# Attention of a two-layer diffusion block: fixed program order, slots per unit, keys before values

## The chip, the cores and the metric

One core of a Trainium2 chip runs the whole program in one launch. The metric is the device time of one execution in microseconds (us), the median over several executions.

## What is computed

A block of two layers works on 512 noisy latent tokens and, in the first layer only, on 256 context tokens, with 1024 channels in fp32. Each layer makes one input projection and splits it into branches; the branch that the change touches is the attention, with 8 heads of 64 channels:

```python
def context_attention(q, k, v):
    s = jnp.einsum('bqhd,bkhd->bhqk', q, k).astype(jnp.float32) * (NA_HEAD_DIM ** -0.5)
    p = jax.nn.softmax(s, axis=-1).astype(v.dtype)
    return jnp.einsum('bhqk,bkhd->bqhd', p, v)
```

A latent query sees a window of 8 x 16 latent positions, with a bias by relative position and rotary q and k, and all 256 context keys in the same softmax; a context query sees the context alone. The other branches are a pooling over windows (A) and a gating unit u * (W_s LN(v) + b) on chunks of 128 positions (B). The three branches are projected, merged by gates, projected again and added to the stream; a squared-ReLU MLP follows.

## The kernel before

Every product is made of three fp32r matmuls (high x high, high x low, low x high), so a weight or an activation is first split into two parts: ScalarE copies the high part (`cp`, L127) and VectorE subtracts it from the value (`sub`, L121). Tokens lie along the free axis: an input projection of one block of 128 channels (`proj`, L451) is 24 pairs of matmuls, one of 512 columns for the latents and one of 256 for the context; where the context isn't needed (q and gates in the second layer) the second one is left out.

The attention takes the heads in four pairs. A unit is one block of 128 queries of one pair: four latent and two context units per pair in the first layer (24 units), four latent ones in the second (16 units). A latent unit goes through these steps:

- `scores`: 12 matmuls on 64 rows (L696) into a PSUM tile of two banks; on VectorE a maximum over the context part (L704), for each of the two heads the bias added with a running maximum (L708), and the sign turned (L710); on ScalarE two exponentials (L712); on VectorE the reciprocal (L714) and the scaling (L716, one per head).
- `turn`: 8 transposes of the weights (L728) in two PSUM banks, and of each the copy (L127) and the subtraction (L121).
- `values`: 8 matmuls (L743), then two copies (L127) and four additions (L752, L753).

A context unit has 6 matmuls of scores, 4 transposes and 4 matmuls of values, and no bias.

While one pair's units run, the projections of the next pair's values, keys and queries (in this order) run between them. `stream` yields them in chunks of six matmuls, and `fill(t)` takes chunks for t us. What these projections leave to do: the rotary step `rope_in` (four ScalarE copies, L640, that exchange halves of the heads; POOL L641 and L645, VectorE L644; the split), the transposes of the values (`v_out`, L625, in the one-bank ring `xring` that the transposes and the values' products of the units use too), the bias tables (`bias_make`, six POOL additions, L679, fed by 16 transfers of `bias_load`), and the second parts of the weights' splits. Part of it stands in the queue `bulk`, of which `drain(SLOT)` takes some 1.9 us of work once per unit, in the midst of `scores`. After the last pair's projections the stream makes six gates. The scheduler of the tile framework is free to move instructions within each engine's program against the order in which they are written. Branch B's product (`gate_mix`, L524) and branch A's (`pool_out`, L512) stand ahead of the attention, behind the projections of u.

## Time and profile before

| | us |
|---|---|
| three timed runs | 1980.58 median (1973.89 to 1982.14) |
| the profiled execution | 1971.65 |
| its span on the core | 1969.9 |
| TensorE busy (PE) | 1924.8, 98% of the span, 11298 instructions |
| VectorE busy (DVE) | 1113.8, 57% |
| ScalarE busy (ACT) | 780.7, 40% |
| GpSimd busy (POOL) | 91.2, 5% |
| chain that ended last | PE 85%, DVE 5%, ACT 5%, issue 2%, POOL 1%, DMA 1% |

The chain goes back from the last instruction, at each step to what released it, and tells which engine the end waits for. Busy time of PE is an upper bound of its work, because a matmul that waits in the pipe counts as busy. In the profile the attention of the first layer lies from about 137 to 335 us and that of the second from about 1254 to 1394 us; the openings with u, branch A and branch B stand just ahead of each.

### The profile page before, as it was taken

The numbers are of one execution on the slowest core, as the hardware profiler recorded it, in microseconds if no ns is written. First come the engines' busy times: TensorE is split into PE (matmuls) and PEld (weight loads), VectorE is DVE, ScalarE is ACT, GpSimd is POOL, SyncE is SP. The second block draws the span as 40 slices with busy tenths as digits, with TensorE's granted clock in tenths as the row PEclk, the third lists the DMA queues.
The fourth block names the chain that finished last, engine by engine and source line by source line (L and its number), as shares of the span: only waits on it lengthen the run. The fifth ranks groups of instructions, "written<-read, shape, count | busy, mean of one in ns | idle before, by whom it ended". The sixth has DMA issues, their size and how long they took to land.

```text
span 1969.9 us, 27864 instructions
## 1 busy us (share of the span) xinstructions
PE 1924.8 (98%) x11298; PEld 1657.4 (84%) x11298; DVE 1113.8 (57%) x1865; ACT 780.7 (40%) x1197; POOL 91.2 (5%) x94
## 2 busy tenths in 40 slices
PE   7999999999999999999999999999999999999998
PEld 3887778888888888888888898777888898989898
DVE  6747676755554565644544467577633554434356
ACT  5535565212133431422413445566422443424253
POOL 0023210000000000000000000341000000000000
PEclk9999899999999999999999999999999999999999
DMA  8222111433342333333343334121232222222324
GB/s 324 70 71 75 43 34 44 128 125 125 126 150 65 109 127 123 125 128 128 129 129 123 102 118 133 47 86 44 75 97 97 96 96 89 94 96 97 96 90 136
DMA packets 63440, 206.25 MB, mean 105 GB/s; under 512 B 7888, under 2 KB 14032, under 8 KB 63312
## 3 DMA queue, kind: packets, MB, share of 16 engines
q1 hardware_dynamic: 63312, 204.48, 31.6%
q8 instruction: 89, 1.46, 0.3%
q14 instruction: 39, 0.32, 0.0%
HBM read 202.35 MB, written 2.10 MB: 104 GB/s over the span
## 4 chain that ended last, share of the span: by engine, by line
PE 85%; DVE 5%; ACT 5%; issue 2%; POOL 1%; DMA 1%; SPq 0%; POOLq 0%; DVEq 0%; ACTq 0%
PE psum L237 68%; PE psum L451 11%; ACT arena_r L127 2%; DVE arena_r L121 1%; PE psum L728 1%; PE psum L743 1%; ACT arena_f L640 1%; PE psum L394 1%; PE psum L696 1%; DMA arena_f<-in_w_mod 1%; ACT arena_f L712 1%; ACT arena_f L127 1%; DVE arena_f L716 1%; POOL arena_f L679 1%; DVE arena_f L118 1%
## 5 line engine op out<-in xcount | busy, mean ns | idle before, releaser
L237 PE MATMUL psum<-arena_r 128*128 128x512 f32 (+1 forms) x8016 | 1370.3, 333 | 1.6 <-DVE arena_f L882 0.9
L237 PEld LDWEIGHTS psum<-arena_r 128*128 128x128 f32 x8016 | 1209.6, 188 | 159.5 <-DVE arena_r L121 1.6
L127 ACT ACTIVATE arena_r<-arena_f 128x1024 fp32r<-128x1024 f32 (+4 forms) x393 | 371.4, 950 | 985.1 <-PE psum L237 782.1
L121 DVE TENSOR_TENSOR arena_r<-arena_f,arena_r 128x1024 fp32r<-128x1024 f32 (+4 forms) x393 | 426.7, 1088 | 274.2 <-ACT arena_r L127 257.3
L451 PE MATMUL psum<-arena_r 128*128 128x512 f32 x1776 | 368.4, 357 | 0.0
L451 PEld LDWEIGHTS psum<-arena_r 128*128 128x128 f32 x1776 | 286.5, 190 | 45.7 <-issue 0.4
L911 DVE SCALAR_TENSOR_TENSOR arena_f<-psum,arena_f 128x512 f32<-128x512 f32 (+1 forms) x128 | 78.3, 633 | 256.1 <-PE psum L237 256.0
L263 DVE SCALAR_TENSOR_TENSOR arena_f<-arena_f 128x1024 bf16<-128x1024 f32 x128 | 156.5, 1222 | 1.4
L963 DVE COPY arena_f<-psum 128x2 f32<-128x2 f32 x64 | 10.3, 160 | 186.9 <-PE psum L237 186.9
L118 DVE TENSOR_TENSOR arena_f<-arena_f 128x768 f32<-128x768 f32 (+8 forms) x103 | 70.0, 681 | 17.4 <-ACT arena_f L274 14.2
L121 DVE TENSOR_TENSOR arena_r<-psum,arena_r 128x512 fp32r<-128x512 f32 (+2 forms) x96 | 61.5, 653 | 19.7 <-ACT arena_r L127 18.5
L127 ACT ACTIVATE arena_r<-psum 128x512 fp32r<-128x512 f32 (+2 forms) x96 | 53.7, 570 | 45.6 <-PE psum L728 25.3
L127 ACT ACTIVATE arena_f<-psum 64x128 f32<-64x128 f32 (+5 forms) x119 | 49.9, 435 | 48.8 <-PE psum L743 19.4
L966 ACT ACTIVATE arena_f<-arena_f 128x512 f32<-128x512 f32 x96 | 59.4, 651 | 11.3 <-DVE arena_f L124 11.3
L712 ACT ACTIVATE arena_f<-psum,arena_f 128x512 f32<-128x512 f32 (+1 forms) x80 | 50.9, 642 | 28.5 <-DVE arena_f L710 28.3
L696 PE MATMUL psum<-arena_r 64*128 64x256 f32 x432 | 48.3, 308 | 7.5 <-ACT arena_f L712 5.4
L728 PE MATMUL psum<-arena_f 128*128 128x128 f32 x288 | 46.2, 285 | 9.0 <-DVE arena_f L753 4.4
L696 PEld LDWEIGHTS psum<-arena_r 64*128 64x128 f32 x432 | 35.1, 186 | 21.7 <-ACT arena_f L712 10.1
L124 DVE TENSOR_TENSOR arena_f<-psum,arena_f 128x768 f32<-128x768 f32 (+1 forms) x64 | 52.2, 816 | 0.0
L728 PEld LDWEIGHTS psum<-arena_f 128*128 128x128 f32 x288 | 32.1, 143 | 20.6 <-DVE arena_f L716 7.8
L882 DVE SCALAR_TENSOR_TENSOR arena_f<-arena_f,psum 128x768 f32<-128x768 f32 (+1 forms) x48 | 39.2, 819 | 17.5 <-PE psum L237 17.1
L679 POOL TENSOR_TENSOR arena_f<-arena_f 128x256 f32<-128x256 f32 x48 | 48.8, 1050 | 3.7 <-DMA arena_f<-in_rpb 3.7
(85 smaller groups left out, 806.8 us busy)
## 6 DMA issues: line engine op xcount, KB each, us to landing
arena_f<-in_w_ff SPq DMA_DIRECT2D x144, 512.0 KB
arena_f<-in_w_in SPq DMA_DIRECT2D x84, 512.0 KB
arena_f<-in_w_modT SPq DMA_DIRECT2D x80, 512.0 KB
arena_f<-in_w_mod SPq DMA_DIRECT2D x16, 512.0 KB
arena_f<-in_w_br SPq DMA_DIRECT2D x16, 512.0 KB
arena_f<-in_w_o SPq DMA_DIRECT2D x16, 512.0 KB
arena_f<-in_rpb SPq DMA_DIRECT2D x128, 30.6 KB
arena_f<-in_xt SPq DMA_DIRECT2D x8, 384.0 KB
```

The lines of the kernel that those rows point to most:

```text
L118: V.tensor_tensor(out=o, in0=a, in1=b, op=ALU.add)
L121: return V.tensor_tensor(out=o, in0=a, in1=b, op=ALU.subtract)
L127: S.activation(out=o, in_=a, func=AF.Copy)
L237: T.matmul(ps_out[:, c0:c1], a, b[:, c0:c1], start=(i == 0), stop=(i == 3 * n - 1))
L263: V.scalar_tensor_tensor(out=junk.f.bitcast(BF16), in0=r.f, scalar=1.0, in1=cb.f[:, s * D:(s + 1) * D], op0=ALU.mult, op1=ALU.mult, accum_ ...
L451: T.matmul(o[:, c0:c1], w[x][:, k, :], ax[k][y][:, c0:c1], start=(i == 0), stop=(i == 23))
L679: G.tensor_tensor(out=tab4[:, hh, y, :].rearrange("q (a k) -> q a k", k=8), in0=view, in1=mask.f[:, y * 256:(y + 1) * 256].rearrange("q (a ...
L696: T.matmul(so[:, hh * 512 + c0:hh * 512 + c0 + 256], a.r[pr, qs], b.r[pr, ks], start=(j == 0), stop=(j == 2))
L712: S.activation(out=pr[:, hh, 0:w], in_=s3[:, hh, 0:w], func=AF.Exp, bias=one[2][hh], accum_out=one[3][hh])
L728: T.transpose(x[:, j * P:(j + 1) * P], pr[:, hh, b * P:(b + 1) * P], ident.f)
L911: V.scalar_tensor_tensor(out=hv(k, c0, c1), in0=o[:, c0:c1], scalar=mcol(l, j, k, s), in1=hv(k, c0, c1), op0=ALU.mult, op1=ALU.add)
L966: S.activation(out=r.f[:, c0:c1], in_=r.f[:, c0:c1], func=AF.Relu, bias=b.f[:, s_:s_ + 1])
```

## The change

All instructions from u's projection to the end of the attention are held in program order on VectorE, ScalarE, GpSimd and TensorE, each engine by itself (`InOrder`). The order of the projections of a pair becomes keys, queries, values. The written order becomes a slot per unit: the next unit's scores, 0.9 us of projection, this unit's transposes, the next one's exponentials, 2.4 us of projection (1.8 beside a context unit), this unit's values, the next one's scaling, this unit's additions, the queue, half of the slot's other projection, the queue again, the other half. The queue is split in two: `soon` holds what a projection leaves to do, in small items with a cost on ScalarE and on VectorE and with the number of their tile, and `weights` the second parts of the weights' splits; `need` runs items of old tiles at once. The rotary step is queued in four items, the bias additions one by one behind those of the keys, the transposes of the values in three. The values' transposes write into the PSUM tile of their own projection and no longer into `xring`. The queries get the opposite sign, so the scores are negative, the maximum is a minimum, the exponential has scale -1, and L710 is gone. `gate_mix` and `pool_out` stand between chunks of the projections of u and of the first keys, in a PSUM ring of their own.

```diff
-CTXW = 0.5
-TAIL = 2.0
-SLOT = 1.9
+CTXW = 0.55
+LEAD = 0.9
+GAP = {"lat": 2.4, "ctx": 1.8}
+QUEUE = {"lat": (2.2, 1.5), "ctx": (1.3, 1.0)}
...
+class InOrder:
+    def __init__(self, tc, nc, eng, on):
+        self.tc, self.nc, self.eng, self.on, self.seen = tc, nc, eng, on, None
+
+    def settle(self):
+        done = self.nc.cur_bb.bb.instructions
+        if self.seen is not None:
+            i = len(done) - 1
+            while i >= self.seen and done[i].engine != self.eng.engine:
+                i -= 1
+            if i >= self.seen:
+                self.tc.keep_in_program_order(Last(done[i]))
+        self.seen = len(done) if self.on[0] else None
...
+    V, S, G, T = (InOrder(tc, nc, e, pin) for e in (nc.vector, nc.scalar, nc.gpsimd, nc.tensor))
+    nr, nf = 31300, 24400
...
-            for m in (14 + p, 10 + p, 6 + p):
+            for m in (10 + p, 6 + p, 14 + p):
...
+    gring = PRing([4, 6], 2)
...
+        def drain(act, dve):
+            first = True
+            while act > 0 and dve > 0 and (soon or weights):
+                if soon and not (soon[0][2] and not first):
+                    ca, cd, _, f, _ = soon.popleft()
+                elif weights:
+                    ca, cd, _, f = weights.popleft()
+                else:
+                    return
+                first = False
                 f()
-                t -= c
+                act -= ca
+                dve -= cd
+
+        def need(tag):
+            while any(it[4] <= tag for it in soon):
+                soon.popleft()[3]()
...
+        pin[0] = True
+        run(proj(2, segs, mm_a, lambda o: nat_in(ut[0].f, o)))
         split(swh, swl, sw.f)
-
-        for i in range(2):
-            for part in range(len(segs)):
-                gate_mix(i, part)
-        pool_out(1)
-        for b in (pwh, pwl, *dh, *dl):
-            b.free()
+        g = proj(3, segs, mm_a, lambda o: nat_in(ut[1].f, o))
+        run(g, 3)
+        pool_out(0)
+        run(g, 2)
+        gate_mix(0, 0)
+        run(g, 2)
+        if not last:
+            gate_mix(0, 1)
+        run(g)
...
+            return [(0.8, 0.0, False, copy)] + [(0.5, 0.6, gi != 2, partial(v_out, p, gi, o)) for gi in (0, 2, 1)]
...
-            x = xring.next()
+            x = o[:, 512:1024] if gi == 2 else o[:, 0:512]
...
-            sc = 1.0 if which == "k" else 0.125
+            sc = 1.0 if which == "k" else -0.125
...
+            items = [(1.2, 0.0, False, partial(swap, 0)), (1.5, 0.0, False, partial(swap, 1)),
+                     (0.0, 1.1, False, turned), (0.6, 0.65, True, halves)]
+            if which == "k":
+                items += [(0.0, 0.0, False, partial(bias_make, p, hh, y)) for hh in range(2) for y in range(3)]
+            return items
...
-            V.tensor_scalar(out=two[2], in0=two[top], scalar1=-1.0, scalar2=None, op0=ALU.mult)
             for hh in range(2):
-                S.activation(out=pr[:, hh, 0:w], in_=s3[:, hh, 0:w], func=AF.Exp, bias=one[2][hh], accum_out=one[3][hh])
-            drain(SLOT)
-            V.reciprocal(out=two[4], in_=two[3])
+                S.activation(out=pr[:, hh, 0:w], in_=s3[:, hh, 0:w], func=AF.Exp, bias=one[low][hh], scale=-1.0,
+                             accum_out=one[2][hh])
...
+        def scaled(pr, w, one, two):
+            V.reciprocal(out=two[3], in_=two[2])
...
+        def gathered(p, kind, qt, o):
...
+                if p:
+                    need(last_tile[p - 1] - 2)
+                if p:
+                    bias_load(p)
+                for i, t in enumerate(proj(10 + p, [LAT, CTX], mm_a, lambda o: rope_in(p, "k", o))):
                     if p and i == HEADK:
                         yield HEAD
-                        bias_load(p)
-                for i, t in enumerate(proj(10 + p, [LAT, CTX], mm_a, lambda o: rope_in(p, "k", o))):
                     yield t
-                    if p and i == 5:
-                        bias_make(p)
-                    if i in (1, 3, 5):
-                        v_out(p, i // 2)
                 yield from proj(6 + p, segs, mm_a, lambda o: rope_in(p, "q", o))
+                yield from proj(14 + p, [LAT, CTX], mm_a, lambda o: v_in(p, o))
+                last_tile[p] = tiles[0] - 1
...
+        run(main, 2)
+        gate_mix(1, 0)
+        run(main, 3)
+        if not last:
+            gate_mix(1, 1)
+        pool_out(1)
+        run(main, 2)
+        for b in (pwh, pwl, *dh, *dl):
+            b.free()
+        open_attention()
+        bias_load(0)
         queued[0] = True
+        while not held[0]:
+            due[0] = 0.0
+            fill(2.5)
+            drain(2.5, 1.6)
...
+                sc = scores(*nxt)
+            fill(LEAD)
+            t = turn(*soft)
+            if nxt:
+                ex = exponentials(*sc)
+            fill(GAP[u[1]])
             if i % per == 0:
-                held[0] = False
-                due[0] = 0.0
-                span = 24 * (3 * n + 2 * (N - n)) / 2400.0 if p < 3 else 3.9 * per
-            fill(span / wsum * (1.0 if u[1] == "lat" else CTXW) - TAIL if (i + 1) % per else 1e9)
-            t = turn(*soft)
-            if i + 1 < len(units):
-                soft = scores(*units[i + 1])
-            fill(TAIL)
-            values(*u, *t)
-        drain(1e9)
+                need(last_tile[u[0]])
+            o = values(*u, *t)
+            if nxt:
+                soft = scaled(*ex)
+            gathered(*u, o)
+            drain(*QUEUE[(nxt or u)[1]])
+            fill((share - LEAD - GAP[u[1]]) / 2)
+            drain(*QUEUE[(nxt or u)[1]])
+            fill((share - LEAD - GAP[u[1]]) / 2)
...
```

Of the 40 instructions that are gone all are L710; on the other engines the counts are the same. The first place is TensorE in the first layer, before the change, at the first units (L451 is a projection, L696 the scores, L728 the transposes; the first six of twelve scores are left out):

```order
L696 MATMUL psum<-arena_r 128x256 [waits DVE_49,Activation_49]
L696 MATMUL psum<-arena_r 128x256 x4
L728 MATMUL psum<-arena_f 128x128 [waits DMAHW1_49,DMAHW0_49,DVE_49]
L728 MATMUL psum<-arena_f 128x128 x2
L728 MATMUL psum<-arena_f 128x128 [waits Pool_49]
L696 MATMUL psum<-arena_r 128x256
L451 MATMUL psum<-arena_r 128x512
L451 MATMUL psum<-arena_r 128x256
L451 MATMUL psum<-arena_r 128x512
L728 MATMUL psum<-arena_f 128x128 [waits DVE_49]
L728 MATMUL psum<-arena_f 128x128 [waits Pool_49]
L728 MATMUL psum<-arena_f 128x128 x2
```

and a slot of a latent unit after the change (L495 is a projection, L751 the scores, L788 the transposes, L803 the values; a slot goes on with further projections):

```order
L751 MATMUL psum<-arena_r 128x256 [waits Activation_49] x2
L751 MATMUL psum<-arena_r 128x256 x10
L495 MATMUL psum<-arena_r 128x512
...
L788 MATMUL psum<-arena_f 128x128 [waits DVE_49]
L788 MATMUL psum<-arena_f 128x128 x3
L788 MATMUL psum<-arena_f 128x128 [waits DVE_49,Activation_49]
L788 MATMUL psum<-arena_f 128x128 x3
L495 MATMUL psum<-arena_r 128x512
...
L803 MATMUL psum<-arena_r 128x256 [waits DVE_49]
L803 MATMUL psum<-arena_r 128x256 x3
L803 MATMUL psum<-arena_r 128x256 [waits DVE_49]
L803 MATMUL psum<-arena_r 128x256 x3
```

Before, the scheduler let one of the twelve scores stand behind the first four transposes and set the other four transposes behind three projection matmuls; now a unit's scores are one row of twelve, its transposes one row of eight, with 6 projection matmuls between them and 12 before the values.

The second place is VectorE in the first layer, before. L704, L708 and L710 belong to the scores, L714 and L716 to the softmax, L121 to splits, L752 and L753 to the additions, L644 and L651 to the rotary step:

```order
L704 TENSOR_REDUCE arena_f<-psum 128x2 [waits PE_49]
L644 SCALAR_TENSOR_TENSOR arena_f<-psum,arena_f 128x512 [waits Activation_49]
...
L651 SCALAR_TENSOR_TENSOR arena_r<-psum,arena_r 128x256 [waits Activation_49]
L710 TENSOR_SCALAR arena_f<-arena_f 128x2 [waits DVE_49]
L121 TENSOR_TENSOR arena_r<-arena_f,arena_r 128x512 [waits Activation_49]
L752 TENSOR_TENSOR arena_f<-psum,arena_f 64x128 [waits Activation_49]
L753 TENSOR_TENSOR arena_f<-psum,arena_f 64x128 [waits DVE_49]
L714 RECIPROCAL arena_f<-arena_f 128x2 [waits Activation_49]
L752 TENSOR_TENSOR arena_f<-psum,arena_f 64x128 [waits Activation_49]
L716 TENSOR_SCALAR arena_f<-arena_f 128x512 [waits DVE_49]
L716 TENSOR_SCALAR arena_f<-arena_f 128x512
L753 TENSOR_TENSOR arena_f<-psum,arena_f 64x128 [waits DVE_49]
```

and after the change (L758 and L762 scores, L147 splits, L774 and L776 softmax, L818 additions, L706 and L709 the rotary step):

```order
L758 TENSOR_REDUCE arena_f<-psum 128x2 [waits PE_49]
L762 ISA psum,arena_f<-psum,arena_f 128x256 [waits DVE_49]
...
L147 TENSOR_TENSOR arena_r<-psum,arena_r 128x4x128 [waits Activation_49] x2
L774 RECIPROCAL arena_f<-arena_f 128x2 [waits Activation_49]
L776 TENSOR_SCALAR arena_f<-arena_f 128x512 [waits DVE_49]
L776 TENSOR_SCALAR arena_f<-arena_f 128x512
L818 TENSOR_TENSOR arena_f<-psum,arena_f 64x128 [waits PE_49,Activation_49]
L818 TENSOR_TENSOR arena_f<-psum,arena_f 64x128
L818 TENSOR_TENSOR arena_f<-psum,arena_f 64x128 [waits DVE_49] x2
L706 SCALAR_TENSOR_TENSOR arena_f<-psum,arena_f 128x512 [waits Activation_49]
L709 SCALAR_TENSOR_TENSOR arena_r<-psum,arena_r 128x256 [waits Activation_49]
```

The sign's instruction is gone, the additions of a unit stand together behind the next one's scaling, and the rotary step comes behind them, where the queue is emptied.

## Rows read from the trace of the kernel before

**Rows 1.** Windows of stages; columns: us, busy of each engine, granted clock, DMA share, GB/s.
```profile
137.00:335.00 198.00, 185.60 (x1161) 151.12 (x1160) 142.85 (x357) 113.85 (x252) 37.83 (x35) 0.97 0.16 48
335.00:352.00 17.00, 17.00 (x99) 14.80 (x99) 3.19 (x5) 3.95 (x6) 0.00 (x0) 1.00 0.20 63
1254.00:1394.00 140.00, 134.19 (x854) 109.58 (x855) 108.35 (x265) 91.39 (x187) 33.45 (x30) 1.00 0.20 63
1179.00:1254.00 75.00, 72.03 (x372) 60.34 (x370) 48.48 (x81) 36.93 (x55) 11.94 (x14) 1.00 0.34 106
```
**Rows 2.** PE's groups from 137 to 335: busy, mean ns | idle before, releasers.
```profile
L451 PE MATMUL psum<-arena_r 128*128 128x512 f32 x291 | 112.3, 418 | 0.0
L451 PE MATMUL psum<-arena_r 128*128 128x256 f32 x291 | 84.1, 289 | 0.0
L696 PE MATMUL psum<-arena_r 64*128 64x256 f32 x240 | 29.1, 314 | 4.5 <-ACT arena_f L712 4.4
L728 PE MATMUL psum<-arena_f 128*128 128x128 f32 x156 | 26.4, 292 | 5.7 <-DVE arena_f L716 2.7 <-DVE arena_f L753 2.5
L743 PE MATMUL psum<-arena_r 128*128 128x256 f32 x156 | 24.9, 293 | 2.2 <-DVE arena_f L753 1.1 <-DVE arena_r L121 0.9
L625 PE MATMUL psum<-arena_f 128*128 128x128 f32 x27 | 4.5, 274 | 0.0
```
**Rows 3.** PE's timeline from 1346 to 1349: start us, us.
```profile
1346.04 1.04 PE L728 MATMUL psum<-arena_f 128*128 128x128 f32 x8
1347.01 0.98 PE L696 MATMUL psum<-arena_r 64*128 64x256 f32 x12
1347.91 1.43 PE L451 MATMUL psum<-arena_r 128*128 128x512 f32 x5
```
**Rows 4.** PE's timeline from 268 to 271.
```profile
268.20 0.66 PE L728 MATMUL psum<-arena_f 128*128 128x128 f32 x4 [0.41 <-DVE arena_f L716]
268.79 0.38 PE L696 MATMUL psum<-arena_r 64*128 64x256 f32 x1
...
269.69 0.39 PE L696 MATMUL psum<-arena_r 64*128 64x256 f32 x2
270.00 1.20 PE L451 MATMUL psum<-arena_r 128*128 128x512 f32 x5
```
**Rows 5.** PE's groups from 1254 to 1394.
```profile
L451 PE MATMUL psum<-arena_r 128*128 128x512 f32 x279 | 86.3, 404 | 0.0
L451 PE MATMUL psum<-arena_r 128*128 128x256 f32 x120 | 34.1, 284 | 0.0
L696 PE MATMUL psum<-arena_r 64*128 64x256 f32 x192 | 19.2, 301 | 3.0 <-ACT arena_r L127 1.8 <-ACT arena_f L712 0.9 <-DVE arena_r L121 0.2
L728 PE MATMUL psum<-arena_f 128*128 128x128 f32 x120 | 18.2, 278 | 3.3 <-DVE arena_f L753 1.9 <-DVE arena_f L716 1.3
L743 PE MATMUL psum<-arena_r 128*128 128x256 f32 x116 | 18.0, 292 | 1.1 <-DVE arena_r L121 1.1
```
**Rows 6.** A window within layer 0's attention, columns as in rows 1.
```profile
205.00:220.00 15.00, 12.65 (x63) 9.97 (x63) 8.19 (x25) 6.29 (x16) 2.59 (x2) 0.77 0.08 33
```
**Rows 7.** VectorE's and ScalarE's groups from 137 to 335, columns as in rows 2.
```profile
L121 DVE TENSOR_TENSOR arena_r<-psum,arena_r 128x512 fp32r<-128x512 f32 x42 | 28.6, 688 | 8.5 <-ACT arena_r L127 7.7
L127 ACT ACTIVATE arena_r<-psum 128x512 fp32r<-128x512 f32 x42 | 24.7, 597 | 21.4 <-PE psum L728 15.9 <-DVE arena_f L710 2.9 <-DVE arena_f L753 1.3
L640 ACT ACTIVATE arena_f<-psum 32x512 f32<-32x512 f32 x24 | 14.2, 592 | 0.4
L710 DVE TENSOR_SCALAR arena_f<-arena_f 128x2 f32<-128x2 f32 x24 | 6.0, 251 | 0.3
L716 DVE TENSOR_SCALAR arena_f<-arena_f 128x512 f32<-128x512 f32 x32 | 14.6, 496 | 0.2
```
**Rows 8.** Timeline of POOL and of VectorE from 155 to 170.
```profile
159.51 5.98 POOL L679 TENSOR_TENSOR arena_f<-arena_f 128x256 f32<-128x256 f32 x6
162.44 1.48 DVE L716 TENSOR_SCALAR arena_f<-arena_f 128x512 f32<-128x512 f32 x2
```

More of the change, by code (lines that the diff above doesn't have):

```diff
@@ L453, in proj @@
                 yield 3 * sum(c1 - c0 for c0, c1 in sg) / 2400.0
-            after(o)
+            items = after(o) or []
+            if queued[0]:
+                soon.extend((*it, u) for it in items)
+            else:
+                for it in items:
+                    it[3]()
         def run(g, steps=None):
@@ new lines, in rope_in, with swap @@
+            buf = {}
+            def swap(half):
+                if half == 0:
+                    buf["x"] = xsr.next()
+                xs = buf["x"]
+                for g in (2 * half, 2 * half + 1):
+                    gg = g ^ 1
+                    S.activation(out=xs.f[32 * g:32 * g + 32, :], in_=o[32 * gg:32 * gg + 32, 0:NL], func=AF.Copy, scale=sc)
+                if half == 1:
+                    G.tensor_tensor(out=xs.f, in0=xs.f, in1=sinb.f, op=ALU.mult)
+                    if nn == N:
+                        S.activation(out=hi.r[:, NL:N], in_=o[:, NL:N], func=AF.Copy, scale=sc)
@@ L855, in build @@
-        drain(1e9)
+        weight = {"lat": 1.0, "ctx": CTXW}
+        wsum = sum(weight[u[1]] for u in units[:per])
+        need(last_tile[0] - 1)
+        ex = exponentials(*scores(*units[0]))
+        held[0] = False
+        due[0] = 0.0
+        fill(2.5)
+        drain(*QUEUE["lat"])
+        fill(2.5)
+        soft = scaled(*ex)
+        drain(*QUEUE["lat"])
+        for i, u in enumerate(units):
+            nxt = units[i + 1] if i + 1 < len(units) else None
+            share = 4.0 * weight[u[1]]
+            if nxt:
+                if i % per == per - 1:
+                    fill(1e9)
+                    held[0] = False
+                    due[0] = 0.0
+                    need(last_tile[nxt[0]] - 1)
+                span = 24 * (3 * n + 2 * (N - n)) / 2400.0 if nxt[0] < 3 else 5.1 * wsum
+                share = span / wsum * weight[nxt[1]]
+                sc = scores(*nxt)
[4 more added lines that the diff above has]
+            fill(GAP[u[1]])
+            if i % per == 0:
+                need(last_tile[u[0]])
+            o = values(*u, *t)
+            if nxt:
+                soft = scaled(*ex)
+            gathered(*u, o)
[3 more added lines that the diff above has]
+            fill((share - LEAD - GAP[u[1]]) / 2)
```

148 lines of the change are left out of this document (72 added, 76 removed).

## The prediction

> **What bounds the kernel now.** I read the windows of the stages first [rows 1]. TensorE (PE) is busy nearly throughout, so the end moves only by what TensorE does in the stretch that is changed. In 335 to 352 us, where almost only projections run, it works without a gap: 99 matmuls in 17.00 us, 0.172 us each. In the two attentions it is idle for 198.00 − 185.60 = 12.4 us and 140.00 − 134.19 = 5.8 us. That is the lower bound of what is lost there, for a matmul that waits in the pipe is busy too: its groups [rows 2, 5] show a mean of 0.418 us for a projection of 512 columns and 0.29 us for a transpose, far over what they take in a row. So I price the instructions at their spacing in unbroken rows and call the rest lost.
>
> Spacing: the pair of 512 and 256 columns averages 0.172, so by columns 0.229 and 0.114. Eight transposes from 1346.04 to the next row's start at 1347.01 give 0.121 each; twelve scores from there to 1347.91 give 0.075 [rows 3]. The products with the values have 256 columns: 0.114. A small group costs something besides: from 268.20 to 270.00 stand 8 transposes in two rows and 3 scores between them [rows 4], which is 1.80 us for 8 × 0.121 + 3 × 0.075 = 1.19, so 0.30 for each of the two score groups.
>
> First layer, 198 us [rows 1, 2]: 582 projections × 0.172 = 100.1; 240 scores × 0.075 = 18.0; 156 transposes × 0.121 = 18.9; 156 values × 0.114 = 17.8; 27 transposes of values × 0.121 = 3.3; together 158.1. With one score group per unit, 24 × 0.30 = 7.2 more: 165.3. Lost: 32.7 us. Second layer, 140 us [rows 1, 5]: 279 × 0.229 = 63.9; 120 × 0.114 = 13.7; 192 × 0.075 = 14.4; 120 × 0.121 = 14.5; 116 × 0.114 = 13.2; 27 transposes of values, as in the first layer, 3.3; with 16 × 0.30 = 4.8 it is 127.8. Lost: 12.2 us. **In all 44.9 us are to be had at most**, 2.3% of the span; matmuls missing from the records make it less.
>
> What are they? The score groups that were split: the order of the kernel has 58 of them, 38 and 20, where the change has 40, so 18 × 0.30 = 5.4 us. The clock: the first layer's mean is 0.97, so 0.03 × 198 = 5.9 us; one fall is in 205 to 220 us at 0.77 [rows 6], 0.23 × 15 = 3.4 us, which is the lower of the two levels (1.2 of 2.4 GHz) for nearly half of the window, in a stretch where TensorE was idle for 2.35 of 15 us. The other 33.6 us are waits: the groups name ScalarE's exponentials for the scores (4.4 us), VectorE's scaling (2.7) and additions (2.5) for the transposes [rows 2]. They are short waits behind an order in which what TensorE takes next has just been started elsewhere.
>
> **The change part by part.**
>
> *The slot* removes most of these waits if each step's cover is longer than what it waits for. Values wait for two copies and two subtractions of the transposes. After the fourth transpose one copy (0.597) and two subtractions (0.688 each) must pass [rows 7], 1.97 us; TensorE has four more transposes and 12 projections in between, 0.48 + 2.06 = 2.5 us. So 0.5 us to spare. The transposes wait for the exponentials and the scaling of scores that were made a slot earlier. A latent slot takes 28.5 projections (582 over 16 latent units and 8 context units at 0.55), 4.9 us, and 0.90 + 0.30 + 0.97 + 0.91 for the unit, 8.0 us; the softmax's work on two engines is some 5 us of it. This holds on average; where the queue stands in between, some waits stay. I take a quarter of the 33.6, 8.4 us, so 25.2 come back. The ends are all and none.
>
> *One score group per unit*: 5.4 us back. *The clock*: fewer gaps should spare falls; I take half, 3.0 us, with 0 and 5.9 as ends.
>
> *The sign (L710)*: 40 × 0.251 = 10.0 us of VectorE are gone [rows 7]. They lie beside TensorE's work; in the slot they would be hidden by the same 8 us. Nothing on its own, unless VectorE bounds (below). The minimum, the mask's sign and the exponential's scale change no duration.
>
> *Keys, queries, values*: the values are needed last, at a pair's first product, so they come last; the keys' rotary step gets one more tile (48 matmuls, 8.3 us) of cover. In the second layer the last pair has no later pair behind it, and there the third group of value transposes follows the second without projections between: it waits for a copy and a subtraction, 0.6 + 0.7. I charge 1.3 us, between 0 and 2.6.
>
> *The values' transposes in the projection's own PSUM tile* leave `xring` to the units; the tile is held longer, but the tile after next is not begun for 8.3 us, and what it waits for is forced through the queue first. I charge nothing; if that cover is gone, it is one wait of 1.3 us for each of 8 tiles at most.
>
> *The openings*: branch B's products between projection chunks. TensorE is idle for 75.00 − 72.03 = 3.0 us of the second layer's opening [rows 1]; I take 1.0 us, between 0 and 3. The bias transfers are issued earlier, at the start of the keys' projection; DMA is busy for 0.16 to 0.34 of these stages, so nothing waits for them. POOL has the same instructions, singly.
>
> Sum: 25.2 + 5.4 + 3.0 − 1.3 + 1.0 = **33.3 us less**, 1971.65 − 33.3 = 1938.4 for an execution such as the profiled one. The three timed runs stood 2.2, 8.9 and 10.5 above it, the median 8.9. I set the forecast half way, 4.5 above: **1943 us**, 1.9% under the median. All to be had, with the opening, is 44.9 + 3 = 47.9: 1924. A time tells itself from no change at about 0.5%, 9.9 us.
>
> **The rivals.**
>
> *A. VectorE becomes the bound.* It is busy 142.85 us of 198 and 108.35 of 140 [rows 1]; without the sign 136.8 and 104.3. In stages of 165 and 128 us that is 83% and 82%, more than the 72% and 77% that it reaches now, and its order is fixed, so a late subtraction holds the next unit's scores. If its share can't rise over 77%, the stages end at 177 and 135 us, 26 us of gain; if over 72% in the first, at 190, 13 us. Middle 20, with the opening 21: 1955. For it: subtractions are what the values wait for. Against: the waits named most are ScalarE's. Chance 0.17.
>
> *B. POOL's additions hold VectorE.* The 24 table additions of a layer now come singly among the units' work. Two scalings took 1.48 us while six additions ran in 5.98 us on POOL [rows 8], where two usually take 2 × 0.496 = 0.99 [rows 7]: 0.49 us more. At 0.5 per addition VectorE gets 12 us more per layer, and at 77% the stages end at 192 and 150, no gain: 1976. At a full 1.0 they end at 208 and 166: 2007. The additions ran beside VectorE before the change as well, so 0.04.
> The Trainium skill, "SBUF — State Buffer", section "Who interferes with whom", says that a VectorE instruction with two SBUF inputs, or in a two-port mode, and a GpSimd instruction that reads SBUF shut each other out, the second blocking until the first is done. By that rule the full 1.0 us would be the price, and the sum would turn into the loss just given; the row shows about a quarter of it per scaling, so I weigh it low.
>
> *C. Slower: ScalarE's fixed order.* The queue's items now stand in ScalarE's program ahead of the next copies. The second emptying comes 5 projections, the scores, 6 projections and four transposes before the first copy: 0.9 + 1.2 + 1.0 + 0.5 = 3.6 us. A rotary step's four exchanges are 4 × 0.592 = 2.4 us [rows 7], and an emptying may overshoot its 2.2 us by the 1.5 of its last item: 3.7. With the 0.5 spare a slot stands still once ScalarE has over 4.1 us. If old waits and split groups go (39.0 us) and each of 40 units waits s, the change decides at s = 0.98 and is slower by 0.5% from 1.22; at 1.5 it is 1971.65 − 39 + 60 + 4.5 = 1997. Against: ScalarE is busy 113.85 of 198 us, 4.7 per unit. Chance 0.07.
>
> *D. The order was not what cost.* The waits may be set by the chain scores, softmax, transposes, values itself, and move instead of going. Then the split groups alone come back, less the new 1.3: 1971.65 − 4.1 + 4.5 = 1972. The projections between the steps speak against it. Chance 0.10.
>
> **The numbers.** Forecast 0.62, A 0.17, B 0.04, C 0.07, D 0.10. Faster by over 0.5% (under 1970.7): all of the forecast, nearly all of A, a third of D: 0.81. Slower (over 1990.5): most of C, half of B: 0.08. Within: 0.11. Range: from 1922, all to be had, to 1973, which takes in A and most of D; left out are C, B and some of either end, 0.18.
>
> **What would show it.** In the profile after: the first attention near 170 to 175 us and the second near 130, TensorE's idle time there under 6 us, its granted clock at 0.98 or more; mean durations of transposes and values nearer 0.2 than 0.29; score groups of 12. For A: VectorE over 80%, TensorE's waits naming L147 (subtraction) alone. For B: scalings over 0.7 us beside POOL. For C: waits of transposes and values that name ScalarE's copies, behind exchanges. It is wrong if the two stages together shrink by less than 12 us.

## The result and the profile after

| | before | after |
|---|---|---|
| median of the timed runs, us | 1979.55 (1973.89 to 1982.14) | 1949.06 (1945.91 to 1951.51) |
| the profiled execution, its span | 1971.65, 1969.9 | 1945.91, 1944.0 |
| ratio after to before | | 0.9849, 95% interval 0.9822 to 0.9875 |

The change is 30 us faster, the two profiled executions differ by 25.7 us. To compare stages with the same work, I cut each attention from its first scores to a fixed matmul behind it (1279 matmuls in the first layer in either kernel; in the second the window before is four matmuls, some 0.4 us, short). Windows of the kernel before, columns as in rows 1:

```profile
137.30:355.80 218.50, 206.09 (x1279) 168.98 (x1279) 149.28 (x365) 120.33 (x262) 37.53 (x34) 0.97 0.16 50
1254.30:1411.50 157.20, 151.66 (x939) 124.06 (x940) 117.82 (x284) 98.71 (x200) 33.45 (x30) 1.00 0.20 63
```

and of the changed one, with two shorter windows, ending at the end of the projections, that are used for prices below:

```profile
138.80:336.70 197.90, 188.89 (x1279) 160.68 (x1279) 152.80 (x352) 119.55 (x264) 37.35 (x30) 1.00 0.16 49
1232.70:1386.40 153.70, 147.16 (x943) 122.97 (x943) 119.95 (x273) 97.57 (x205) 38.20 (x30) 1.00 0.17 53
138.70:333.80 195.10, 186.09 (x1264) 158.27 (x1263) 150.96 (x350) 117.93 (x263) 37.35 (x30) 1.00 0.16 49
1232.60:1383.70 151.10, 144.56 (x933) 120.98 (x932) 117.25 (x271) 95.91 (x203) 38.20 (x30) 1.00 0.17 53
```

The first attention is 20.6 us shorter and the second 3.5, together 24.1; the first layer's clock went from 0.97 to 1.00. The rest of the 25.7 lies outside: the first scores come 1.5 us later, the part between the attentions is 2.5 us shorter, the end 0.8. Between the attentions, 190 us of projections (410 to 600) hold 1098 matmuls in these two profiles and 1077 or 1078 in some others at the same granted clock of 1.00, among them that of rope_apart below, which has the changed kernel's order of instructions; this moves a time by some 5 us from one execution to another.

How the 24.1 us came about is only in part to be seen as idle time. TensorE's idle time in the two windows fell from 12.4 + 5.5 to 9.0 + 6.5 us, by 2.4. The clock gave some 6.6 (0.03 of 218.5). The other 15 lie in time that counts as busy; waits within the pipe and split score groups both count there, and no run here tells them apart.

TensorE's groups in the changed kernel's first attention, 138.7 to 333.8 us, answer to [rows 2]:

```profile
L495 PE MATMUL psum<-arena_r 128*128 128x512 f32 x337 | 124.7, 408 | 0.0
L495 PE MATMUL psum<-arena_r 128*128 128x256 f32 x337 | 94.1, 279 | 0.0
L803 PE MATMUL psum<-arena_r 128*128 128x256 f32 x160 | 25.0, 294 | 5.3 <-DVE arena_r L147 4.9
L788 PE MATMUL psum<-arena_f 128*128 128x128 f32 x160 | 21.9, 275 | 0.3 <-DVE arena_f L776 0.3
L751 PE MATMUL psum<-arena_r 64*128 64x256 f32 x240 | 20.6, 299 | 0.0
L677 PE MATMUL psum<-arena_f 128*128 128x128 f32 x27 | 4.1, 279 | 3.4 <-ACT arena_f L153 3.4
```

and two of the groups of the second, 1232.6 to 1383.7 us, to [rows 5]:

```profile
L803 PE MATMUL psum<-arena_r 128*128 128x256 f32 x128 | 19.0, 290 | 1.6 <-DVE arena_r L147 1.4
L677 PE MATMUL psum<-arena_f 128*128 128x128 f32 x29 | 4.5, 278 | 3.9 <-DVE arena_r L147 3.9
```

In the first layer scores wait no more (4.5 us before), and transposes hardly (0.3 us instead of 5.7). What is left are the values behind a subtraction (L803, 5.3 and 1.6 us) and the values' own transposes (L677, 3.4 and 3.9). Before, these two waited 2.2 and 0.0 us in the first layer: of the 9.9 us of visible waiting that went, 6.5 turned up here. One slot shows both. TensorE, first layer (start, us):

```profile
205.84 0.98 PE L751 MATMUL psum<-arena_r 64*128 64x256 f32 x12
206.75 1.33 PE L495 MATMUL psum<-arena_r 128*128 128x512 f32 x6
207.93 1.03 PE L788 MATMUL psum<-arena_f 128*128 128x128 f32 x8
208.72 3.36 PE L495 MATMUL psum<-arena_r 128*128 128x512 f32 x18
212.68 1.34 PE L803 MATMUL psum<-arena_r 128*128 128x256 f32 x8 [0.60 <-DVE arena_r L147]
215.52 0.88 PE L677 MATMUL psum<-arena_f 128*128 128x128 f32 x6 [1.49 <-ACT arena_f L153]
```

VectorE in the same slot:

```profile
207.91 0.69 DVE L706 SCALAR_TENSOR_TENSOR arena_f<-psum,arena_f 128x512 f32<-128x512 f32 x1 [1.17 <-ACT arena_f L698]
208.52 0.41 DVE L709 SCALAR_TENSOR_TENSOR arena_r<-psum,arena_r 128x256 fp32r<-128x256 f32 x1
209.26 1.23 DVE L147 TENSOR_TENSOR arena_r<-arena_f,arena_r 128x1024 fp32r<-128x1024 f32 x1 [0.33 <-ACT arena_r L153]
210.41 0.68 DVE L758 TENSOR_REDUCE arena_f<-psum 128x2 f32<-128x512 f32 x1
...
211.94 1.28 DVE L147 TENSOR_TENSOR arena_r<-psum,arena_r 128x512 fp32r<-128x512 f32 x2
```

The next unit's scores end at 206.82, but their minimum (L758) begins at 210.41: VectorE first waits for ScalarE's exchanges (L698) and works off the queue. This unit's subtractions, written behind the minimum and the bias additions, come at 211.94 and the values wait in spite of 18 projection matmuls of cover. Then the values' transposes stand right behind the copy that they read, since a short slot ahead of a context unit leaves no projection between the two emptyings.

### The profile page after: what moved, and what is told of

It is laid out like the page before. It is cut to its first block, busy times and chain, and to the rows that moved or that the text cites. A ratio compares the mean times of both kernels' runs of the same rounds, so it can differ in the third digit from the quotient of the medians.

```text
span 1944.0 us, 27767 instructions
## 1 busy us (share of the span) xinstructions
PE 1903.0 (98%) x11298; PEld 1651.5 (85%) x11298; DVE 1112.5 (57%) x1825; ACT 773.2 (40%) x1197; POOL 101.7 (5%) x94
## 4 chain that ended last, share of the span: by engine, by line
PE 88%; DVE 5%; ACT 4%; issue 1%; DMA 1%; SPq 0%; DVEq 0%; ACTq 0%
PE psum L263 70%; PE psum L495 11%; PE psum L803 2%; DVE arena_r L147 2%; PE psum L421 1%; PE psum L788 1%; ACT arena_f L153 1%; PE psum L751 1%; DMA arena_f<-in_w_mod 1%; ACT arena_r L153 1%; ACT arena_f L698 1%; DVE arena_f L818 1%; DVE arena_f L758 1%; DVE arena_f L144 1%; DVE psum L762 1%
## 5 line engine op out<-in xcount | busy, mean ns | idle before, releaser
L263 PEld LDWEIGHTS psum<-arena_r 128*128 128x128 f32 x8016 | 1211.9, 189 | 154.8 <-ACT arena_f L884 0.5
L153 ACT ACTIVATE arena_r<-arena_f 128x1024 fp32r<-128x1024 f32 (+3 forms) x393 | 371.0, 949 | 939.6 <-PE psum L263 803.5
L147 DVE TENSOR_TENSOR arena_r<-arena_f,arena_r 128x1024 fp32r<-128x1024 f32 (+4 forms) x393 | 427.8, 1091 | 246.3 <-ACT arena_r L153 237.3
L495 PE MATMUL psum<-arena_r 128*128 128x512 f32 x1776 | 360.7, 354 | 0.3 <-DVE arena_r L147 0.3
L495 PEld LDWEIGHTS psum<-arena_r 128*128 128x128 f32 x1776 | 283.3, 189 | 45.2 <-DVE arena_r L147 0.5
L289 DVE SCALAR_TENSOR_TENSOR arena_f<-arena_f 128x1024 bf16<-128x1024 f32 x128 | 156.3, 1221 | 1.4
L147 DVE TENSOR_TENSOR arena_r<-psum,arena_r 128x512 fp32r<-128x512 f32 (+2 forms) x96 | 59.2, 651 | 15.1 <-ACT arena_r L153 14.7
L818 DVE TENSOR_TENSOR arena_f<-psum,arena_f 64x128 f32<-64x128 f32 x160 | 46.4, 290 | 22.6 <-ACT arena_f L153 18.9
L803 PE MATMUL psum<-arena_r 128*128 128x256 f32 x288 | 44.0, 292 | 6.9 <-DVE arena_r L147 6.3
L803 PEld LDWEIGHTS psum<-arena_r 128*128 128x128 f32 x288 | 38.1, 189 | 14.5 <-DVE arena_r L147 12.6
L988 DVE SCALAR_TENSOR_TENSOR arena_f<-arena_f,psum 128x768 f32<-128x768 f32 (+1 forms) x48 | 39.0, 819 | 19.4 <-PE psum L263 19.1
L1073 ACT ACTIVATE arena_f<-arena_f 128x768 f32<-128x768 f32 (+1 forms) x64 | 47.5, 742 | 2.0
```

The lines of the kernel that those rows point to most:

```text
L147: return V.tensor_tensor(out=o, in0=a, in1=b, op=ALU.subtract)
L153: S.activation(out=o, in_=a, func=AF.Copy)
L263: T.matmul(ps_out[:, c0:c1], a, b[:, c0:c1], start=(i == 0), stop=(i == 3 * n - 1))
L289: V.scalar_tensor_tensor(out=junk.f.bitcast(BF16), in0=r.f, scalar=1.0, in1=cb.f[:, s * D:(s + 1) * D], op0=ALU.mult, op1=ALU.mult, accum_ ...
L495: T.matmul(o[:, c0:c1], w[x][:, k, :], ax[k][y][:, c0:c1], start=(i == 0), stop=(i == 23))
L803: T.matmul(o[:, hh * 256:(hh + 1) * 256], vhl[p].r[:, v0:v0 + P], pt.r[:, t0:t0 + 256], start=(b == 0), stop=(b == nb - 1))
```

## The experiments

Each was timed against the kernel before in five rounds. Times are medians; "stages" are the two attentions of the one profiled execution, cut as above (after the change 197.9 and 153.7 us). Dots in an edit mark lines left out.

**free_order.** The scheduler free, the written slots kept.

```diff
-        pin[0] = True
+        pin[0] = False
```

> The changed kernel with the scheduler free again (no engine held in program order; the written slots stay). Theory: the written slots made the gain, since they put cover between the steps, so the time stays near the changed kernel, 1944 to 1956 us. Rival: holding the order is what counts; then at least half of the 30 us are lost again, over 1964 us.

1942.07 us, ratio 0.9815 (0.9793 to 0.9837): no loss; the runs (1940.18 to 1944.91) lie under all of the changed kernel's, though the intervals of the ratios touch. TensorE's order is nearly the same, with 40 score groups; in the first layer the values' transposes (L677) now hardly wait (0.1 us) and the values 4.4 us. The written slots made the gain; holding the order did not, by this edit.

**before_pinned.** The old written order, held.

```diff
...
+        pin[0] = True
         for i in range(2):
             g = proj(2 + i, segs, mm_a, lambda o: nat_in(ut[i].f, o))
...
         queued[0] = False
+        pin[0] = False
...
```

> The kernel before, with its own written order, held in that order on the four engines from u's projections to the end of the attention. Theory: this joins the split score groups (18 x 0.30 = 5.4 us) and may spare a fall of the clock, but the waits of the old slots stay: 1966 to 1978 us. Rival (holding the order is the gain): 1945 to 1957 us. Second rival (queued work now stands ahead of what TensorE waits for): slower than before, over 1985 us.

2120.32 us, ratio 1.0708 (1.0683 to 1.0734): the second rival, and by 140 us. Windows of the two attentions, and three of the longest waits in the first:

```profile
151.10:432.70 281.60, 219.05 (x1279) 183.85 (x1279) 154.94 (x375) 121.47 (x264) 31.46 (x28) 0.87 0.11 37
1332.80:1553.30 220.50, 173.28 (x943) 141.92 (x943) 123.13 (x289) 98.67 (x204) 33.55 (x29) 0.87 0.13 41
```

```profile
DVE arena_r L146 <- ACT arena_r L152: 82.8, 44, 16.1
ACT arena_f L738 <- DVE arena_f L736: 51.8, 21, 3.7
ACT arena_f L152 <- DVE arena_f L779: 42.4, 24, 3.6
```

Exponentials (L738) wait for the sign (L736), copies (L152) for additions (L779), and subtractions (L146) for copies: each engine's next instruction waits for the other engine, and what is written behind it waits too. Of 126 us more in the two stages, 110 − 18 = 92 are idle time of TensorE more than before, and 0.13 of 502 us, 65 us, went with the clock, against 7 before (the two overlap). Most of the rest lies in the first opening: the first scores come at 151.1 us instead of 137.3. A written order that the scheduler used to repair is far worse when it is held.

**turn_first.** The minimum behind this unit's subtractions (`lowest` holds the minimum and the bias additions).

```diff
...
-                ex = exponentials(*sc)
+                ex = exponentials(*lowest(*sc))
```

> The changed kernel, with the next unit's minimum and bias additions written behind this unit's transposes, copies and subtractions. Theory: the values wait because the subtractions stand behind the next unit's minimum on VectorE; with them first, the values' idle time before L803 (5.3 us in the first layer, 1.6 in the second) falls under 2 us, and the time by 3 to 9 us, to 1940 to 1946 us. Rival: ScalarE's copies behind queued work set those waits; then the idle time stays over 4 us and the time within 2 us of the changed kernel.

1975.90 us, ratio 0.9979 (0.9963 to 0.9994): 27 us slower than the changed kernel, where 3 to 9 us less were expected. Its second attention:

```profile
L791 PE MATMUL psum<-arena_f 128*128 128x128 f32 x128 | 18.3, 283 | 6.1 <-ACT arena_r L153 3.0 <-DVE arena_f L779 2.2 <-DVE arena_f L821 1.0
L806 PE MATMUL psum<-arena_r 128*128 128x256 f32 x128 | 18.1, 284 | 0.0
L677 PE MATMUL psum<-arena_f 128*128 128x128 f32 x30 | 5.0, 296 | 8.8 <-DVE arena_r L147 8.8
```

The values' wait went as expected (1.6 to 0.0; 5.3 to 1.8 in the first), so the theory of that wait holds. But the exponentials come later and all that stands behind them on ScalarE too: the values' transposes wait 8.8 us, up to 3.6 at a time, transposes 6.1, and the granted clock is 0.98 and 0.97 in the two stages (208.3 and 166.8 us). The order of the change is the better of the two.

**vt_apart.** No transposes of values at the second emptying where nothing stands between (the last item of a rotary step bears the same mark and is held back with them).

```diff
...
-            drain(*QUEUE[(nxt or u)[1]])
...
+            drain(*QUEUE[(nxt or u)[1]], apart)
...
```

> The changed kernel, but where no projection stands between the two emptyings of a slot, the second one begins with no transposes of values. Theory: three of the six long waits before the values' transposes go (1.49, 1.49, 2.01 us), 3 to 6 us less than the changed kernel, 1943 to 1946 us, and the idle time before them falls from 7.3 us to under 3.5. Rival: the wait moves to the values' products, which then name the same copy or subtraction; the time is the same within 2 us.

1948.01 us, ratio 0.9841 (0.9817 to 0.9865): the same as the changed kernel. Before L676, idle time fell from 3.4 to 0.4 us in the first layer, whose stage is 3.1 us shorter. In the second it fell from 3.9 to 1.9, and projections (L494) began to wait for the weights' splits:

```profile
L494 PE MATMUL psum<-arena_r 128*128 128x512 f32 x348 | 105.2, 406 | 3.7 <-DVE arena_r L147 3.7
L676 PE MATMUL psum<-arena_f 128*128 128x128 f32 x36 | 5.4, 277 | 1.9 <-DVE arena_r L147 1.9
```

The theory's idle time held (7.3 to 2.3 us), its gain did not: in the second layer the wait moved, though not to where the rival had it.

**sign_back.** The sign's instruction again (with maximum, positive queries and additions).

```diff
...
+            V.tensor_scalar(out=two[4], in0=two[low], scalar1=-1.0, scalar2=None, op0=ALU.mult)
...
```

> The changed kernel with the sign's instruction put back (positive queries, maximum, 40 small VectorE operations between the bias additions and the exponentials). Theory of the prediction: VectorE has room, so the time is that of the changed kernel within 3 us (1946 to 1952 us). Rival (VectorE's fixed row is what the values wait for, so each slot's subtractions come 0.17 to 0.25 us later): 4 to 10 us slower, 1953 to 1959 us, and the values' idle time over 9 us in the two layers instead of 6.9.

1960.29 us, ratio 0.9894 (0.9868 to 0.9920), 11 us slower than the changed kernel; stages 206.4 and 159.0. Its runs lie far apart, from 1953.63 to 1967.61, and the last is the profiled one. The values' waits, first and second attention:

```profile
PE psum L804 <- DVE arena_r L147: 10.5, 12, 1.4
PE psum L804 <- DVE arena_r L147: 3.8, 6, 2.0
```

The values wait twice as long (14.3 for 6.3 us), as the rival said: 0.2 us in front of each slot's subtractions (the sign took 4.6 us for 24 in the first attention). And the clock fell to 0.98 and 0.99. Two of the six runs took 1953.63 and 1954.02 us at a mean clock of 0.998, the profiled one has 0.992: the 11 us hold the clock's falls besides the waits.

**before_signless.** That part of the change alone, in the kernel before.

```diff
...
-            V.tensor_scalar(out=two[2], in0=two[top], scalar1=-1.0, scalar2=None, op0=ALU.mult)
...
```

> The kernel before with the sign alone changed (negative queries, minimum, exponential with scale -1; 40 small VectorE operations gone), its own order otherwise. In the changed kernel putting the sign back cost 11 us. Theory: that instruction stands on the row minimum, bias, exponential, and in front of the subtractions, in either order; then the kernel before gains 4 to 12 us by this edit alone, 1968 to 1977 us. Rival: it costs only where VectorE's order is held; then nothing here, 1978 to 1984 us.

1966.49 us, ratio 0.9937 (0.9914 to 0.9959): 13 us, a little over what the theory gave. In the profiles the first attention is 11.5 us shorter and the second 2.9 longer (160.1). The window of the first, and scores and transposes in its 137 to 335 us:

```profile
138.50:345.50 207.00, 195.54 (x1279) 162.92 (x1278) 145.53 (x341) 118.82 (x262) 36.36 (x34) 1.00 0.17 53
L696 PE MATMUL psum<-arena_r 64*128 64x256 f32 x240 | 25.2, 306 | 0.7 <-ACT arena_f L711 0.7
L727 PE MATMUL psum<-arena_f 128*128 128x128 f32 x156 | 23.7, 279 | 9.2 <-DVE arena_f L715 5.1 <-DVE arena_f L752 3.8
```

The scores' wait for the exponentials is gone (4.5 to 0.7 us), transposes wait more (5.7 to 9.2), and the clock is 1.00 in the first attention. TensorE's idle time in the stage hardly changes (12.4 to 11.5 us); the clock gives 6.6 of the 11.5. Before, this stood there (TensorE, then ScalarE):

```profile
206.58 2.28 PE L451 MATMUL psum<-arena_r 128*128 128x512 f32 x12
210.63 0.50 PE L696 MATMUL psum<-arena_r 64*128 64x256 f32 x2 [1.77 <-ACT arena_f L712]
208.84 0.63 ACT L127 ACTIVATE arena_r<-arena_f 128x512 fp32r<-128x512 f32 x1 [2.78 <-POOL arena_f L645]
209.80 0.69 ACT L712 ACTIVATE arena_f<-psum,arena_f 128x512 f32<-128x512 f32 x1
```

The scores have one PSUM tile, so the next unit's wait until the exponentials have read it. The sign did not hold these exponentials: it was done at 207.60. The scheduler had put a rotary step's copy ahead of them, and ScalarE stood there for 2.78 us until POOL was done. Without the sign the exponentials come ahead of that copy, and ScalarE's waits for POOL's sum (L645) in 137 to 335 us fall (before, then this run):

```profile
ACT arena_r L127 <- POOL arena_f L645: 9.5, 6, 2.8
ACT arena_r L127 <- POOL arena_f L645: 1.8, 4, 0.6
```

So the edit came with another order on ScalarE and without the falls of the clock; that the instruction's own 0.25 us on the path is worth 13 us, as the theory had it, is not shown. The kernel still has 60 score groups, two more than before, and gains 13 us.

**one_emptying.** The queue once per slot, twice the amount.

```diff
-            drain(*QUEUE[(nxt or u)[1]])
-            fill((share - LEAD - GAP[u[1]]) / 2)
-            drain(*QUEUE[(nxt or u)[1]])
-            fill((share - LEAD - GAP[u[1]]) / 2)
+            drain(*(2 * x for x in QUEUE[(nxt or u)[1]]))
+            fill(share - LEAD - GAP[u[1]])
```

> The changed kernel with the queue emptied once per slot, behind the additions, for twice the amount, and no second time. Theory: ScalarE and VectorE then meet a longer row of queued work ahead of the next unit's copies and minimum, while nothing stands in the second half of the slot; TensorE waits more for copies and subtractions: 4 to 20 us slower than the changed kernel, 1953 to 1969 us. Rival: the place of queued work does not matter as long as the sum is done in the slot: within 3 us of it.

1959.50 us, ratio 0.9895 (0.9875 to 0.9915), in the theory's range, but not all as it said: the first attention is shorter (194.5 us), the second longer (171.4, clock 0.94), where nine transposes of values stand in a row:

```profile
PE psum L677 <- DVE arena_r L147: 9.9, 3, 4.4
```

**values_first.** The old order of the projections.

```diff
...
-            for m in (10 + p, 6 + p, 14 + p):
+            for m in (14 + p, 10 + p, 6 + p):
...
```

> The changed kernel with the projections of a pair in the old order, values, keys, queries, so that the queries' rotary step must be done at the pair's border. Theory: the values' transposes no longer stand behind their copy at the border (their idle time falls from 7.3 us to under 3), but the scores of a pair's first unit wait for the queries' exchanges and split instead, 2 to 4 us at each of six borders: 3 to 15 us slower than the changed kernel, 1952 to 1964 us. Rival: the order of the three is worth nothing, within 3 us.

The queries' rotary step must be done at a pair's border, and here they are the last of the three. By the code, the next pair's bias table may be loaded before this pair's last additions have read theirs, and then some biases are another pair's. 1995.02 us, ratio 1.0075 (1.0052 to 1.0098): 46 us slower than the changed kernel. The longest of TensorE's waits in its second attention:

```profile
PE psum L751 <- ACT arena_r L153: 12.0, 4, 5.6
PE psum L495 <- DVE arena_r L147: 7.8, 4, 2.2
PE psum L495 <- DVE arena_f L706: 7.3, 3, 2.7
```

At the borders the scores wait up to 5.6 us for a split's copy, that of the queries, which come last: the mechanism of the theory. The price, 46 us, is three times the upper end of the 3 to 15 that I had set, and the scores' 12.0 us are the smaller part of it: projections wait 15.1 us besides, and the second attention takes 188.2 us at a clock of 0.93. How much the table adds is open.

**rope_apart.** VectorE's part of the rotary step in a later emptying.

```diff
-                     (0.0, 1.1, False, turned), (0.6, 0.65, True, halves)]
+                     (0.0, 1.1, True, turned), (0.6, 0.65, True, halves)]
```

> The changed kernel, but VectorE's part of the rotary step begins an emptying of its own, half a slot behind ScalarE's exchanges. Theory: VectorE no longer stands idle for the exchanges ahead of the next unit's minimum and this unit's subtractions, so the values' idle time in the first layer falls from 5.3 us to under 3 and the time by 2 to 5 us, to 1944 to 1947 us. Rival: the values wait for the amount of queued work, not for its place; the idle time stays over 4.5 us and the time within 2 us.

1948.37 us, ratio 0.9838 (0.9818 to 0.9859), and in the first attention TensorE's values wait 5.4 us for the subtractions, where it was 4.9. This run tests neither the theory nor the rival: in both attentions the instructions of VectorE and of ScalarE stand in the same order as in the changed kernel, and VectorE's wait for the exchanges is what it was (L706 behind L698, 7.1 us in the first attention after 7.2). The exchanges are booked at 1.2 + 1.5 = 2.7 us, over the 2.2 that an emptying takes, so the rotary step's part on VectorE began another emptying already. What the run gives is a repetition of the changed kernel, 0.7 us beside it. Whether the values wait for the amount of queued work ahead of the minimum or for VectorE's idle time there stays open.

**opening_block.** Branch B in one block behind u.

```diff
...
+        run(g, 5)
...
         run(g)
+        for i in range(2):
+            for part in range(len(segs)):
+                gate_mix(i, part)
+        pool_out(1)
...
```

> The changed kernel with branch B's products and branch A's second one back in one block behind the projections of u. The prediction gave their place between projections 1.0 us. Theory: 1 to 4 us slower than the changed kernel, 1950 to 1953 us, with more idle time of TensorE ahead of the first scores. Rival: the place is worth nothing (the first scores came 1.5 us later after the change than before): 1946 to 1949 us.

1948.83 us, ratio 0.9848 (0.9823 to 0.9873): the place is worth nothing that these runs can tell.

**v_in_xring.** The values' transposes in the units' ring.

```diff
-            x = o[:, 512:1024] if gi == 2 else o[:, 0:512]
+            x = xring.next()
```

> The changed kernel with the transposes of the values written to the ring xring again. Theory: they take turns with the units' transposes and products, so a unit's step waits for their copy and subtraction, 1.3 us for some of 12 groups in a layer: 2 to 10 us slower than the changed kernel, 1951 to 1959 us. Rival: xring has room, and a projection's tile comes free earlier: within 2 us.

1958.67 us, ratio 0.9896 (0.9875 to 0.9917), 10 us slower; stages 203.6 and 156.3. TensorE's order is the same. In the first attention transposes now wait for the additions (L818) that free the ring, and the values' transposes too:

```profile
PE psum L788 <- DVE arena_f L818: 3.5, 3, 1.2
PE psum L677 <- ACT arena_f L153: 3.4, 3, 1.5
PE psum L677 <- DVE arena_f L818: 1.3, 3, 0.4
```

**free_gap.** free_order with more cover between transposes and values.

```diff
-GAP = {"lat": 2.4, "ctx": 1.8}
+GAP = {"lat": 3.4, "ctx": 1.8}
```

> The changed kernel with the scheduler free (as in the run free_order) and 3.4 in place of 2.4 us of projection between the transposes and the values of a latent unit. Theory: the values' idle time behind subtractions (4.4 and 3.6 us in free_order) falls under 2 us in all, and the time to 1934 to 1940 us, under free_order's 1942. Rival: the projections taken there are missing elsewhere, so transposes or the values' transposes wait in their place: 1942 us or more.

**1930.52 us**, ratio 0.9757 (0.9734 to 0.9780): 18.5 us less than the changed kernel, 49 less than the kernel before, and the best here. Stages 191.1 and 149.4. The longest of TensorE's waits in the first attention:

```profile
PE psum L803 <- DVE arena_r L147: 1.8, 5, 0.7
PE psum L751 <- ACT arena_f L769: 0.5, 1, 0.5
PE psum L788 <- DVE arena_f L818: 0.4, 1, 0.4
```

In the second the values wait 0.3 us; in free_order they waited 4.4 and 3.6. That they waited for want of cover is shown. The projections taken here were hardly missing elsewhere: transposes wait 0.8 and 1.7 us, where it was 0.0 and 0.3.

## Why the prediction was right, and where its sum was off

The direction and the range held, and the mechanism in the main: the waits in front of scores and transposes went, and so did the falls of the clock in the first attention. But of TensorE's visible idle time only 2.4 of 18.0 us went, because values and their transposes wait where they did not before; a sign that the prediction gave, idle time under 6 us, did not come (9.0 and 6.5). By the prediction's own prices the changed kernel still loses 12.5 us in 138.7 to 333.8 (337 pairs 115.9, scores and their groups 25.2, 160 transposes 19.4, 160 values 18.2, the rest 3.9: 182.6 of 195.1), and 7.7 in the second (143.4 of 151.1). So 20.2 of 44.9 us are left; the prediction left 8.4 + 2.9 + 1.3 = 12.6. That is 7.6 too few, the whole distance between the forecast gain of 33.3 us and the 25.7 of the profiled executions; the medians lie 30.5 apart. By terms:

- **The values' transposes** are where the sum failed most: "I charge nothing; if that cover is gone, it is one wait of 1.3 us for each of 8 tiles at most", with 1.3 us for the last pair. The cover is gone at six places, because a slot without projections puts copy and transposes side by side: 3.4 + 3.9 = 7.3 us. Yet the same edit is worth having: undone, it costs 10 us.
- **The values' margin** of 0.5 us was worked out from the copies and subtractions alone. What stands in front of them on VectorE, the queue and the next minimum, takes it up (6.9 us of idle time; turn_first shows the minimum's part); with more cover the time fell by 11.6 us against free_order.
- **The clock**: 3.0 us were taken, all 5.9 came back.
- **The score groups**: 5.4 us, not shown. A kernel with 60 of them was 13 us faster than one with 58; what a split group costs hangs on what it waits for.
- **The sign**: "Nothing on its own" was wrong: 11 us when put back, 13 when taken from the kernel before. Put back, it stands at the head of a fixed row, minimum, bias, sign, subtractions, and the 8 us of a slot don't hide it: the values wait 8.0 us more. In the kernel before it is another matter, since there the scheduler's order changed with it.
- **Prices don't add up**: undoing the sign, the tile, the second emptying and the order of projections one by one costs 11, 10, 10 and 46 us, 77 together, where the whole change gained 30. Each edit's worth depends on the cover that the others leave.
- **The order of the projections**: the keys' cover was named as the use. The border's scores, which need the queries, are what it saves.
- **The opening**: 1.0 us forecast, none measured; the first scores came 1.5 us later.

Of the rivals, D (waits move instead of going) is right for the visible idle time of the first attention, of which two thirds moved, and wrong for the time, 1972 us against 1949.06; free_gap shows that the moved waits give way to more cover. A is half right: VectorE sets the waits that are left, not by its share (151 of 195 us, 77%) but by what stands in front. C needed ScalarE's row; before_pinned and turn_first show that such a convoy exists, 27 to 140 us, but the change's order avoids it. B is small: the scaling's mean rose from 0.496 to 0.593 us, 3 us of VectorE in the layer. Where it meets POOL it can cost more than the prediction's row: two took 2.04 us while POOL's additions ran (VectorE, then POOL):

```profile
147.80 1.23 DVE L147 TENSOR_TENSOR arena_r<-arena_f,arena_r 128x1024 fp32r<-128x1024 f32 x1 [0.34 <-ACT arena_r L153]
151.92 2.04 DVE L776 TENSOR_SCALAR arena_f<-arena_f 128x512 f32<-128x512 f32 x2
147.92 2.25 POOL L707 TENSOR_TENSOR arena_f<-arena_f 128x512 f32<-128x512 f32 x1
150.13 5.40 POOL L735 TENSOR_TENSOR arena_f<-arena_f 128x256 f32<-128x256 f32 x6
```

Alone, two scalings take 0.88 to 0.99 us, so the delay is 1.1. POOL is held up as well: its addition at 147.92 took 2.25 us beside a subtraction with two SBUF inputs that had begun before it, and the one ahead of it 1.29. The Trainium skill, "SBUF — State Buffer", section "Who interferes with whom", has the second of the two blocked until the first is done. The 0.96 us that POOL lost agree with that, as the subtraction still ran for 1.11; for the scalings it would be up to 0.9 us each, an estimate from six additions in 5.40 us, and the 1.1 us here and the 0.49 of rows 8 both lie below that sum. Not every such pair shows it: before the change a subtraction with two SBUF inputs took its usual 0.68 us at 160.33, while POOL's additions of rows 8 ran. The prediction's sums for B are a little low: 192 + 150 is 4 us over 338 and 208 + 166 is 36, which with the 4.5 of the forecast makes 1980 and 2012 for 1976 and 2007.

Another sign that the prediction gave to look for was ill chosen: mean durations of transposes and values stayed at 0.275 and 0.294 us. They are the time in the pipe; the spacing shows the gain.

## What to carry to other kernels

Price a step by what stands in front of it on its engine as well as by what it waits for: a small instruction at the head of a row that is worked through in order is not hidden by the idle time behind it. Write the order with cover between a producer and its reader first, and measure holding it apart from writing it: holding cost 140 us in the old order and gained nothing in the new one. If a wait is left behind a step, give that step more independent work ahead before reordering its engine; here one constant brought 11.6 us (with the scheduler free), where the reordering cost 27 (with the order held). And compare the order of instructions that an edit leaves before its time is explained: in rope_apart it changed nothing, in before_signless more than the edit says.

## What was not expected of the hardware

Where two in-order engines wait for each other, the loss is larger than the idle time: in before_pinned TensorE's granted clock was 0.87 in both attentions, a mean of its two levels, 1.2 and 2.4 GHz, and in one_emptying 0.94 in the second, with waits of up to 4.4 us; 1.00 in the same stage of the changed kernel. A kernel with the same matmuls can pay for its gaps twice.
